# Two unused tiles that move the SBUF pools to multiples of 2048 bytes in a hybrid SSM, convolution and feed-forward layer

## The chip, the cores and the metric

The kernel runs on one core of a Trainium2 chip. The metric is the device time of one execution in microseconds (us), taken as the median over runs. The profile is one execution recorded by the hardware profiler; its times count from the first instruction.

## What is computed

One layer with model width 2048 over 512 positions, in float32, batch 1:

```
h = rms_norm(x, pre_mix_g);  u, v, g = split(h @ w_in)          # 2048 -> 3 x 1024
y_ssm  = s5_mixer(u, ...)          # complex diagonal state space, gelu, y * sigmoid(y @ w_glu)
y_conv = silu(layer_norm(causal_conv31(v * sigmoid(g))))
x = x + rms_norm(concat(y_ssm, y_conv) @ w_out, post_mix_g)     # 2048 -> 2048
h = rms_norm(x, pre_ffn_g)
gate, val = split(causal_conv3(h @ w_up))                       # 2048 -> 2 x 5632
x = x + rms_norm((gelu(gate) * val) @ w_down, post_ffn_g)       # 5632 -> 2048
```

## The kernel before

Activations lie with channels on the 128 partitions and the 512 positions along the free axis, so one tile of 128 channels is 512 float32 numbers, 2048 bytes of each partition. Every large product is done by `gemm`. A weight chunk of 128x1024 float32 (8 blocks of 128x128) is loaded into `wraw`, ScalarE rounds it to fp32r (`wh`, L96) and VectorE takes the rest (`wl`, L97). An activation likewise stands as a high tile and a low tile. For each block TensorE then does three matmuls with 512 columns into one PSUM bank:

```
pe.matmul(ps[m], wh[:, kk, m, :], xh, start=k == 0, stop=False)
pe.matmul(ps[m], wh[:, kk, m, :], xl, start=False, stop=False)
pe.matmul(ps[m], wl[:, kk, m, :], xh, start=False, stop=k == nk - 1)
```

These are L116, L117 and L118. The 512-column operand streamed through the array is called the moving operand; the 128x128 block loaded ahead of it is the weight.

There are 8448 such matmuls. 2112 come before the feed-forward part (input projection, gated linear unit, output projection), with moving tiles in pool `hl16` (name `hl`, slices of 2048 bytes). The feed-forward part has 22 calls for `w_up` with 8 chunks of 24 matmuls, 4224 in all, whose moving tiles are again `hl`; and 44 calls for `w_down` with 2 chunks of 24, 2112 in all, whose moving tiles `hidh` and `hidl` lie in pool `hid`. Calls for `w_up` and `w_down` alternate: after each two `w_up` calls come four of `w_down`.

`wh` and `wl` have two buffers each, `wraw` three. A planner orders the instructions of each engine; weight loads and splits get a higher priority (`WPRI`).

Before the feed-forward part VectorE also does the 31 taps of the convolution (L567), the evacuations and part of the state space work, so that the splits L97 wait in its queue among them. At the end come the last normalization and the stores.

**Where the tiles lie.** Pools are laid one after the other in the order in which they are opened, each tile rounded up to 32 bytes. Ahead of the first lie 16,512 bytes of the program's own. `const` takes 3,808 bytes, so `hl16` starts at 20,320 = 9 x 2048 + 1888. `hl16`, `s16`, `wp` (`wraw`, `wh`, `wl`), `rp` and the first tiles of `t1` (`tmp`) have sizes that are multiples of 2048, so each of their tiles starts at 1888 past a multiple of 2048; a weight block of `wh` or `wl` starts at that plus a multiple of 512. `t1` ends with small tiles (1,152 bytes past a multiple), so the pools behind it, `cp` in the first phase and `hid` in the second, start at 170,976 = 83 x 2048 + 992.

Of the kernel before, what the change touches and what calls it, by code (L numbers as in the profile page):

```python
# [10 lines left out]
F32 = mybir.dt.float32  # L11
# [5 lines left out]
P = 128  # L17
# [39 lines left out]
def layer_kernel(ctx, tc, a, out):  # L57
    nc = tc.nc
    ve, se, ge, pe, sy = nc.vector, nc.scalar, nc.gpsimd, nc.tensor, nc.sync

    const = ctx.enter_context(tc.tile_pool(name="const", bufs=1))
    dram = ctx.enter_context(tc.tile_pool(name="dram", bufs=1, space=bass.MemoryType.DRAM))
    hl16 = ctx.enter_context(tc.tile_pool(name="hl16", bufs=4))
    s16 = ctx.enter_context(tc.tile_pool(name="s16", bufs=2))
# [7 lines left out]
    def tmp():  # L72
        return t1.tile([P, S], F32, name="tmp", bufs=NTMP)
# [53 lines left out]
    def rsqrt_bcast(parts, n, copy=True):  # L127
# [20 lines left out]
        se.copy(out=rb, in_=rps)  # L148
        return rb

    ph1 = ExitStack()
    cp = ph1.enter_context(tc.tile_pool(name="cp", bufs=2, reuse_waits="tile"))

    def k4():
        return cp.tile([P, 1024], F32, name="k4", bufs=3)
# [68 lines left out]
    gpf = cload("post_ffn_g", [P, DK])  # L224
    fcw = cload("ffn_conv_w", [P, 2 * NFF, 3])

    # ---- SSM parameters, states on partitions (group of a pair, state), pairs of groups along the free axis
    uscr = [dram.tile([HC, T, 8, NC], F32, name=f"uscr{m}") for m in range(8)]
    wscr = [dram.tile([2, 16, T, P], F32, name=f"wscr{h}") for h in range(2)]
    bscr = dram.tile([P, 2, NQ, HC], F32, name="bscr")  # L230
# [58 lines left out]
    tt(sh, sh, sh, MUL)  # L289
    ts(sh, sh, -2.0, 1.0, MUL, ADD)  # L290

    # powers of the step: lamr, and lami with the sign turned, by (pair, power)
    lamr = p2.tile([P, NQ, NT], F32, name="lamr")
    lami = p2.tile([P, NQ, NT], F32, name="lami")
    ge.memset(lamr[:, :, 0], 1.0)
# [24 lines left out]
    lpow(1, 2, 2)  # L320
    lpow(1, 3, 4)

    # (step - 1) / eigenvalue
    lr, li = lamr[:, :, 1], sn[:, 0:NQ]
    nr = ts(sm("nr"), lr, -1.0, 1.0, ADD, MUL)
    ab, ab2 = sm("ab"), sm("ab2")
# [20 lines left out]
    tt(tA, tA, tB, SUB)  # L347
    tt(coi, tA, rd, MUL)

    # times powers of the step: columns to rows, and spread over the channels of a group  # L350
    cf = pp.tile([P, 2, NQ, T], F32, name="cf")
    cx = pp.tile([P, NQ, T], F32, name="cx")

# [22 lines left out]
    prep.close()  # L376
    cv = ph1.enter_context(tc.tile_pool(name="cv", bufs=1, reuse_waits="tile"))

    # discretized B
    bsb = k4().rearrange("p (r q h) -> p r q h", r=2, h=HC)  # L380
    bin_ = k4().rearrange("p (r q h) -> p r q h", r=2, h=HC)
    sy.dma_start(out=bin_, in_=a["ssm_b"])
# [12 lines left out]
    for h in range(2):  # L395
# [5 lines left out]
        for mm in range(4):  # L401
# [5 lines left out]
            by = tmp().rearrange("p (q s) -> p q s", q=4)  # L407
# [4 lines left out]
            ve.tensor_tensor(out=w0, in0=w0, in1=bx, op=SUB)  # L412
            ve.tensor_tensor(out=w1, in0=w1, in1=by, op=ADD)

    # C times powers of the step (with the sign of the imaginary part turned)
    for m in range(8):
        ct = cp.tile([P, 2, 4, NT, HC], F32, name="cst", bufs=2)
        cin = p2.tile([P, 2, 4, HC], F32, name="cin")
# [14 lines left out]
            sy.dma_start(out=cscr[m][:, :, gg].rearrange("r p q t -> p r q t"),  # L433
                         in_=ct[PH * gg:PH * gg + PH].rearrange("p r q t h -> p r q (t h)"))

    # ---- input projection: the SSM branch
    def uload(m):
        um = t1.tile([P, S], F32, name="um", bufs=2).rearrange("p (g c) -> p g c", g=8)
        sy.dma_start(out=um, in_=uscr[m].rearrange("h j g c -> (h j) g c"))
        return um  # L440
# [20 lines left out]
    u_evac(pu0, 0)  # L461
    u_evac(gemm(wing[1], xrhs), 4)

    # ---- recurrence over chunks
    ve.memset(st[:, :, :, 0], 0.0)
    lr8 = lam8[:, 0:1, :].broadcast_to([P, 2, NQ])
    for c in range(NC - 1):
# [4 lines left out]
        ve.tensor_tensor(out=sa, in0=sa, in1=st[:, :, :, c + 1], op=ADD)  # L472
        scan_end = ve.tensor_tensor(out=st[:, :, :, c + 1], in0=sa, in1=sx, op=ADD).ins

    # ---- response within a chunk
    kb = s16.tile([P, 4096], F32, name="s16")
    bst = kb[:, 0:1056].rearrange("p (r q h) -> p r q h", r=2, h=HC)
    ge.memset(bst[:, :, NQ, :], 0.0)
# [56 lines left out]
        for i in range(2):  # L535
            sy.dma_start(out=yall[:, m - 1 + i], in_=yscr[m // 2][P * i:P * i + P])

    # ---- input projection: the convolution branch
    csb = cv.tile([P, 8, S], F32, name="csb")

    def vg_evac(ps, i0):
# [28 lines left out]
    for i in range(4):  # L570
        vg_evac(gemm(wing[2 + i], xrhs), 2 * i)

    # ---- SSM branch: operands of the gated linear unit
    yh = hl16.tile([P, 8, S], F32R, name="hl")
    yl = hl16.tile([P, 8, S], F32R, name="hl")
    yc = []
# [4 lines left out]
                         in1=yh[:, m, :].bitcast(F32).rearrange("p (c j) -> p c j", j=T), op=SUB)  # L581
        yc.append(yn)

    # ---- SSM branch: gated linear unit
    zh = hl16.tile([P, 8, S], F32R, name="hl")
    zl = hl16.tile([P, 8, S], F32R, name="hl")
    yrhs = [(yh[:, k, :], yl[:, k, :]) for k in range(8)]
# [10 lines left out]
            se.copy(out=zh[:, m, :], in_=zt)  # L598
            ve.tensor_tensor(out=zl[:, m, :], in0=zt, in1=zh[:, m, :].bitcast(F32), op=SUB)

    # ---- convolution branch: layer norm and swish
    cs = rp.tile([P, S], F32, name="ssq")
    ge.tensor_tensor(out=cs, in0=csb[:, 0], in1=csb[:, 1], op=ADD)
    for i in range(2, 8):
# [21 lines left out]
        se.copy(out=ch[:, i, :], in_=sl)  # L626
        ve.tensor_tensor(out=cl[:, i, :], in0=sl, in1=ch[:, i, :].bitcast(F32), op=SUB)

    # ---- output projection
    yo = [s16.tile([P, 8, S], F32, name="s16") for _ in range(2)]  # L630

    def yt(m):
# [26 lines left out]
    ry = rsqrt_bcast([yss] + last, D, False)  # L659
    ph1.close()  # L660

    # ---- residual, and the norm before the feed-forward part
    hid = ctx.enter_context(tc.tile_pool(name="hid", bufs=8, reuse_waits="tile"))
    t2 = ctx.enter_context(tc.tile_pool(name="t2", bufs=1, reuse_waits="tile"))
    x1scr = dram.tile([P, DK, S], F32, name="x1scr")
# [27 lines left out]
            ge.tensor_tensor(out=xs2, in0=xs2, in1=sq, op=ADD)  # L693
    r2 = rsqrt_bcast([xs2], D)

    # ---- feed-forward part
    fa = [s16.tile([P, 8, S], F32, name="s16") for _ in range(2)]

    def ft(m):
# [150 lines left out]
```

## Time and profile before

| | |
|---|---|
| median of 3 runs | 2148.36 us (2146.53 to 2149.66) |
| profiled execution, span from first to last instruction | 2146.2 us |
| time of the runs' median beyond that span | 2.2 us |
| TensorE busy | 2029.9 us, 95% of the span |
| VectorE busy | 1215.0 us, 57% |
| ScalarE busy | 665.7 us, 31% |
| DMA | 118 GB/s mean |

The profiled execution has its span as its own time; what a run takes beyond it is shown by the third line. Matmuls overlap in the pipeline, so the duration of one (about 0.39 us) is longer than the distance from its start to the start of the next; the distance is what counts.

### The profile page before, as it was taken

Reading aid. Unit: us, or ns where it says so; the run is one execution under the profiler, and the core shown is the slowest. Engines: PE = TensorE matmul, PEld = TensorE weight load, DVE = VectorE, ACT = ScalarE, POOL = GpSimd, SP = SyncE. Lnnn points to the kernel's source line nnn. Section 1 sums busy time; section 2 is a strip of 40 time slices with the busy share of each in tenths; the row PEclk is TensorE's granted clock in tenths of the full one; section 3 lists DMA queues with packets and bytes.
Section 4 is the critical chain, followed back from the end, with each engine's and each line's share of the span. In section 5 each row is a group of like instructions: output and inputs, shape, how many; then the busy total and the mean of one; then the engine's idle time right before and its main releaser. Section 6 shows DMA issues by size and latency. Waiting matters only on the chain.

```text
span 2146.2 us, 23254 instructions
## 1 busy us (share of the span) xinstructions
PE 2029.9 (95%) x9190; PEld 1659.9 (77%) x9190; DVE 1215.0 (57%) x1609; ACT 665.7 (31%) x827; POOL 290.4 (14%) x291
## 2 busy tenths in 40 slices
PE   7767999799997999999999999999999999999995
PEld 6656788677886888888888888888888888888884
DVE  6288999998439552453544535345443464434546
ACT  5111233433535333222312223122231222213233
POOL 6655144303023000000000000000000000000004
PEclk9888999899998999999999999999999999999998
DMA  6785576322423322232223222222232222322242
GB/s 205 170 211 161 202 205 198 95 89 91 174 98 127 109 90 97 98 98 97 91 97 98 98 89 98 98 98 92 96 98 98 98 89 98 98 96 94 95 167 98
DMA packets 111373, 252.36 MB, mean 118 GB/s; under 512 B 28064, under 2 KB 49568, under 8 KB 110752
## 3 DMA queue, kind: packets, MB, share of 16 engines
q1 hardware_dynamic: 106512, 248.77, 36.2%
q10 hardware_dynamic: 4752, 2.11, 0.4%
q8 instruction: 72, 1.18, 0.2%
q14 instruction: 37, 0.30, 0.0%
HBM read 229.67 MB, written 21.17 MB: 117 GB/s over the span
## 4 chain that ended last, share of the span: by engine, by line
PE 72%; DVE 3%; ACT 1%; issue 0%; DVEq 0%; ACTq 0%
PE mm L118 24%; PE mm L116 24%; PE mm L117 24%; DVE hl L685 0%; DVE s L775 0%; DVE s L682 0%; DVE wl L97 0%; DVE hidh L683 0%; PE aux L144 0%; DVE s L776 0%; DVE hidl L683 0%; ACT L137 0%; ACT wh L96 0%; ACT tmp L759 0%; ACT tmp L655 0%
## 5 line engine op out<-in xcount | busy, mean ns | idle before, releaser
L97 DVE TENSOR_TENSOR wl<-wraw,wh 128x1024 fp32r<-128x1024 f32 (+1 forms) x353 | 441.3, 1250 | 777.7 <-ACT wh L96 771.7
L116 PE MATMUL mm<-hl,wh 128*128 128x512 f32 x2112 | 831.9, 395 | 15.2 <-ACT wh L96 9.4
L118 PE MATMUL mm<-hl,wl 128*128 128x512 f32 x2112 | 778.6, 397 | 60.2 <-DVE wl L97 60.2
L117 PE MATMUL mm<-hl,wh 128*128 128x512 f32 x2112 | 831.4, 394 | 0.2 <-DVE hl L685 0.2
L96 ACT CAST wh<-wraw 128x1024 fp32r<-128x1024 f32 (+1 forms) x353 | 370.4, 1050 | 1091.3 <-PE mm L117 1004.7
L118 PEld LDWEIGHTS mm<-hl,wl 128*128 128x128 f32 x2112 | 403.5, 191 | 154.9 <-DVE wl L97 70.1
L116 PEld LDWEIGHTS mm<-hl,wh 128*128 128x128 f32 x2112 | 402.7, 191 | 99.8 <-ACT wh L96 9.8
L117 PEld LDWEIGHTS mm<-hl,wh 128*128 128x128 f32 x2112 | 402.5, 191 | 86.6 <-DVE hl L685 1.4
L117 PE MATMUL mm<-hidl,wh 128*128 128x512 f32 x704 | 277.6, 394 | 0.0
L116 PE MATMUL mm<-hidh,wh 128*128 128x512 f32 x704 | 277.4, 395 | 0.0
L118 PE MATMUL mm<-hidh,wl 128*128 128x512 f32 x704 | 256.6, 395 | 0.0
L761 POOL TENSOR_TENSOR ssq<-ssq,tmp 128x512 f32<-128x512 f32 x11 | 17.3, 1577 | 1394.2 <-ACT tmp L759 1393.7
L567 DVE SCALAR_TENSOR_TENSOR csb<-z,c_conv_w,csb 128x512 f32<-128x512 f32 x210 | 182.9, 930 | 0.0
L116 PEld LDWEIGHTS mm<-hidh,wh 128*128 128x128 f32 x704 | 132.2, 188 | 32.6 <-ACT wh L96 0.5
L118 PEld LDWEIGHTS mm<-hidh,wl 128*128 128x128 f32 x704 | 132.2, 188 | 32.0
L117 PEld LDWEIGHTS mm<-hidl,wh 128*128 128x128 f32 x704 | 132.2, 188 | 31.6
L751 DVE TENSOR_TENSOR s<-mm,s 128x512 f32<-128x512 f32 x160 | 109.9, 691 | 51.1 <-PE mm L118 50.6
L726 DVE SCALAR_TENSOR_TENSOR tmp<-ab,c_ffn_conv_w,tmp 128x512 f32<-128x512 f32 x176 | 125.5, 748 | 0.0
L724 ACT ACTIVATE tmp<-ab,c_ffn_conv_w 128x512 f32<-128x512 f32 x88 | 63.0, 720 | 44.5 <-DVE ab L716 44.5
L716 DVE TENSOR_TENSOR ab<-mm,rr 128x512 f32<-128x512 f32 x88 | 60.4, 689 | 8.2 <-PE mm L118 4.5
L564 POOL TENSOR_TENSOR csb<-csb,pt 128x512 f32<-128x512 f32 x30 | 54.0, 1800 | 53.6 <-ACT pt L563 53.6
L732 ACT CAST hidh<-tmp 128x512 fp32r<-128x512 f32 x44 | 27.2, 621 | 76.6 <-DVE tmp L730 76.6
(212 smaller groups left out, 964.6 us busy)
## 6 DMA issues: line engine op xcount, KB each, us to landing
wraw<-in_ffn_w_up SPq DMA_DIRECT2D x176, 512.0 KB, 3.4
wraw<-in_ffn_w_down SPq DMA_DIRECT2D x88, 512.0 KB, 3.4
wraw<-in_w_in SPq DMA_DIRECT2D x47, 512.0 KB, 5.0
wraw<-in_w_out SPq DMA_DIRECT2D x32, 512.0 KB, 3.4
cst<-cscr SPq DMA_DIRECT2D x16, 576.0 KB, 5.0
cscr<-cst SPq DMA_DIRECT2D x16, 288.0 KB, 4.4
k<-in_ssm_bT SPq DMA_DIRECT2D x8, 512.0 KB, 3.7
um<-uscr SPq DMA_DIRECT2D x16, 256.0 KB, 5.0
```

Of the source, the lines that this page charges most:

```text
L96: se.copy(out=h[:, o], in_=raw[:, o])
L97: ve.tensor_tensor(out=l[:, o], in0=raw[:, o], in1=h[:, o].bitcast(F32), op=SUB)
L116: pe.matmul(ps[m], wh[:, kk, m, :], xh, start=k == 0, stop=False)
L117: pe.matmul(ps[m], wh[:, kk, m, :], xl, start=False, stop=False)
L118: pe.matmul(ps[m], wl[:, kk, m, :], xh, start=False, stop=k == nk - 1)
L564: ge.tensor_tensor(out=csb[:, c, :], in0=csb[:, c, :], in1=pt, op=ADD)
L567: ve.scalar_tensor_tensor(out=csb[:, c, :], in0=zk, scalar=w, in1=csb[:, c, :], op0=MUL, op1=ADD)
L716: ve.tensor_tensor(out=t[:, 2:], in0=ps[j], in1=r2, op=MUL)
L724: se.activation(out=o, in_=t[:, 0:S], func=AF.Copy, scale=fcw[:, c, 0:1])
L726: ve.scalar_tensor_tensor(out=o, in0=t[:, k:k + S], scalar=fcw[:, c, k:k + 1], in1=o, op0=MUL, op1=ADD)
L732: se.copy(out=h, in_=cvt[0])
L751: ve.tensor_tensor(out=ft(m), in0=ps[i], in1=ft(m), op=ADD)
```

## The change

Two pools with one tile each are opened, `lead` with 160 bytes in each partition between `const` and the pools behind it, and `lead2` with 896 bytes behind `t1`. Nothing writes or reads either tile. The pools from `hl16` to `t1` move up by 160 bytes, so that `hl16` starts at 20,480 = 10 x 2048; the pools behind `lead2` move up by 1,056 bytes, to 172,032 = 84 x 2048. `hl`, `wraw`, `wh`, `wl`, `ssq`, `tmp`, `k4` and `hid` tiles then start at multiples of 2048. `um` and `evt`, which lie behind small tiles of `t1`, start at 128 past one; the second `cst` buffer starts at 512 past one; `const` stays where it is. Some comment lines become blank.

```
     const = ctx.enter_context(tc.tile_pool(name="const", bufs=1))
+    lead = ctx.enter_context(tc.tile_pool(name="lead", bufs=1))
+    lead.tile([P, 40], F32, name="lead")
     dram = ctx.enter_context(tc.tile_pool(name="dram", bufs=1, space=bass.MemoryType.DRAM))
     hl16 = ctx.enter_context(tc.tile_pool(name="hl16", bufs=4))
...
+    lead2 = ctx.enter_context(tc.tile_pool(name="lead2", bufs=1))
+    lead2.tile([P, 224], F32, name="lead2")
     ph1 = ExitStack()
     cp = ph1.enter_context(tc.tile_pool(name="cp", bufs=2, reuse_waits="tile"))
```

## Rows read from the trace of the kernel before

**Rows 1.** The page: span, and TensorE's granted clock in 40 slices (tenths).

```profile
span 2146.2 us, 23254 instructions
...
PEclk9888999899998999999999999999999999999998
```

**Rows 2.** The page: chain that ended last, by engine and by line.

```profile
PE 72%; DVE 3%; ACT 1%; issue 0%; DVEq 0%; ACTq 0%
PE mm L118 24%; PE mm L116 24%; PE mm L117 24%; DVE hl L685 0%; DVE s L775 0%; DVE s L682 0%; DVE wl L97 0%; DVE hidh L683 0%; PE aux L144 0%; DVE s L776 0%; DVE hidl L683 0%; ACT L137 0%; ACT wh L96 0%; ACT tmp L759 0%; ACT tmp L655 0%
```

**Rows 3.** Busy time by stretch (start:end, length, engines, granted clock, DMA share, GB/s).

```profile
0.00:500.00 500.00, 420.07 (x2151) 341.04 (x2152) 419.68 (x648) 158.06 (x205) 208.56 (x231) 0.91 0.58 168
500.00:650.00 150.00, 145.34 (x653) 119.79 (x651) 80.78 (x95) 71.06 (x99) 30.76 (x26) 1.00 0.36 123
650.00:712.00 62.00, 52.64 (x219) 41.56 (x220) 52.68 (x67) 28.35 (x44) 23.42 (x15) 0.89 0.40 136
...
760.00:2118.00 1358.00, 1357.98 (x5930) 1112.87 (x5929) 615.15 (x732) 383.59 (x450) 17.34 (x11) 1.00 0.29 98
```

**Rows 4.** Groups by line, 712 to 2118 us: TensorE, `hl` and `hid` matmuls.

```profile
L117 PE MATMUL mm<-hl,wh 128*128 128x512 f32 x1346 | 523.8, 389 | 0.0
...
L117 PE MATMUL mm<-hidl,wh 128*128 128x512 f32 x702 | 276.8, 394 | 0.0
```

**Rows 5.** Timeline of TensorE, `hl` matmuls: first and last of 14.

```profile
760.01 0.39 PE L117 MATMUL mm<-hl,wh 128*128 128x512 f32 x1
...
762.96 0.39 PE L117 MATMUL mm<-hl,wh 128*128 128x512 f32 x1
```

**Rows 6.** Timeline of TensorE, `hid` matmuls: first, second and last of 15 starts.

```profile
936.65 0.39 PE L116 MATMUL mm<-hidh,wh 128*128 128x512 f32 x1
936.88 0.40 PE L117 MATMUL mm<-hidl,wh 128*128 128x512 f32 x1
...
939.92 0.63 PE L118 MATMUL mm<-hidh,wl 128*128 128x512 f32 x2
```

**Rows 7.** Busy time by stretch: one stretch at the lower clock.

```profile
336.50:346.50 10.00, 10.00 (x38) 9.03 (x38) 10.00 (x11) 2.04 (x3) 3.89 (x3) 0.50 0.68 203
```

**Rows 8.** Timeline of TensorE in that stretch, `hl` matmuls: first and last of 9.

```profile
342.83 0.63 PE L116 MATMUL mm<-hl,wh 128*128 128x512 f32 x1
...
346.24 0.57 PE L116 MATMUL mm<-hl,wh 128*128 128x512 f32 x1
```

**Rows 9.** Timeline of TensorE, 64-column matmuls around 336.5 us, first and last.

```profile
335.79 0.28 PE L525 MATMUL aux<-um,k 128*128 128x64 f32 x1
...
336.35 0.60 PE L526 MATMUL aux<-tmp,cst 128*128 128x64 f32 x2
336.74 0.63 PE L525 MATMUL aux<-um,k 128*128 128x64 f32 x2
...
341.43 0.64 PE L526 MATMUL aux<-tmp,cst 128*128 128x64 f32 x2
```

**Rows 10.** Groups by line, TensorE, 0 to 500 us (last column: idle before, releaser).

```profile
L118 PE MATMUL mm<-hl,wl 128*128 128x512 f32 x496 | 190.5, 418 | 51.9 <-DVE wl L97 51.9
```

**Rows 11.** The same, 500 to 650 us.

```profile
L118 PE MATMUL mm<-hl,wl 128*128 128x512 f32 x208 | 74.5, 390 | 3.2 <-DVE wl L97 3.2
```

**Rows 12.** Waits, 712 to 2118 us (total, times, longest).

```profile
ACT wh L96 <- PE mm L117: 809.2, 237, 4.5
DVE wl L97 <- ACT wh L96: 698.9, 201, 4.4
```

**Rows 13.** Groups by line, VectorE, 712 to 2118 us.

```profile
L751 DVE TENSOR_TENSOR s<-mm,s 128x512 f32<-128x512 f32 x158 | 108.5, 691 | 51.1 <-PE mm L118 50.6
L716 DVE TENSOR_TENSOR ab<-mm,rr 128x512 f32<-128x512 f32 x88 | 60.4, 689 | 8.2 <-PE mm L118 4.5 <-ACT rr L148 3.7
L730 DVE TENSOR_TENSOR tmp<-tmp 128x512 f32<-128x512 f32 x44 | 30.3, 691 | 0.1
L734 DVE TENSOR_TENSOR hidl<-tmp,hidh 128x512 fp32r<-128x512 f32 x44 | 30.2, 689 | 9.3 <-ACT hidh L732 9.3
```

More of the change, by code (lines that the diff above doesn't have):

```diff
@@ L61, in layer_kernel @@
     const = ctx.enter_context(tc.tile_pool(name="const", bufs=1))
+    lead = ctx.enter_context(tc.tile_pool(name="lead", bufs=1))
+    lead.tile([P, 40], F32, name="lead")
     dram = ctx.enter_context(tc.tile_pool(name="dram", bufs=1, space=bass.MemoryType.DRAM))
@@ L149, in rsqrt_bcast @@
         return rb
+    lead2 = ctx.enter_context(tc.tile_pool(name="lead2", bufs=1))
+    lead2.tile([P, 224], F32, name="lead2")
     ph1 = ExitStack()
```

## The prediction

> **What bounds the kernel now.** I read the page first. The granted clock is near full in most slices [rows 1], and the chain of work that ended last is made of the three matmul lines of `gemm`, 24% of the span each [rows 2]. The other 28% is mostly the time before 531 us, to which the chain was not followed back.
>
> Then I cut the span into stretches. From 760 to 2118 us TensorE is busy for 1357.98 of 1358.00 us at full clock, VectorE for 615, ScalarE for 384, with a DMA share of 0.29 [rows 3]. The matmul groups there have no idle time before them [rows 4]. So the feed-forward part, two thirds of the time, lasts as long as its matmuls take to follow each other, and nothing else counts. Before 500 us it is mixed: TensorE has 420 us and VectorE 420 us of 500 [rows 3], and 51.9 us of TensorE's idle time end with the split `wl` [rows 10]. From 500 to 650 us TensorE binds again (145 of 150), with 3.2 us of such waits [rows 3, 11].
>
> The change issues no instruction and moves none. It can only act through what an address does to an instruction's time, and the one time that matters is the distance from one matmul to the next. [...]
>
> - moving operand `hl`, full clock: 13 distances from 760.01 to 762.96 us, 2.95/13 = 226.9 ns [rows 5];
> - moving operand `hid`, full clock: 14 distances from 936.65 to 939.92 us, 3.27/14 = 233.6 ns [rows 6];
> [...]
>
> The mean over 760 to 2118 us agrees: 1358/5930 = 229.0 ns [rows 3], against (2 x 226.9 + 233.6)/3 = 229.1.
>
> [...] And `hl` and `hid` matmuls are the same instruction in shape, type, weights and target bank; what differs is where the moving tile lies: 1888 past a multiple of 2048 for `hl`, 992 for `hid`. That place is worth 6.7 ns. [...]
>
> **The change part by part.** `lead` and `lead2` hold 160 and 896 bytes and cost no instruction, no DMA and no wait; there is nothing to hide. Nothing is queued differently on any engine or DMA queue, if the planner's order stays, which I assume.
>
> *Moving operands.* `hl` goes from 1888 to 0, `hid` from 992 to 0. After it no 2048-byte read of either crosses a 2048-byte boundary, where all of them do now. The trace has no 512-column read from such a place, so I bound the distance. Below, by the array: 213.2 ns, half of rows 8. Above, where the excess stays: 226.9 and 233.6. If steps of 6.7 ns are what a bad start adds, an aligned one has none (213.2) or one (about 220). I don't take the lowest: the 64-column matmuls show that not everything halves with the clock. Five distances from 335.79 to 336.35 us give 112 ns at full clock, 22 from 336.74 to 341.43 give 213.2 at half [rows 9], so 112 - 106.6 = 5 ns are left over. I take the middle, 216.7 ns, for both tiles.
>
> The sum by stretch:
>
> - `w_up`: 4224 x (226.9 - 216.7) = 43.1 us. Of these 189 run before 712 us, where TensorE has gaps (52.6 busy of 62, clock 0.89 [rows 3]); their 1.9 us I don't count: 41.2.
> - `w_down`: 2112 x (233.6 - 216.7) = 35.7 us.
> - 500 to 650 us: three lines with about 208 matmuls each [rows 11], 623 x 10.2 = 6.4 us.
> - 0 to 500 us: 1491 matmuls (three lines of about 497 [rows 10]), at most 15.2 us. VectorE is as busy as TensorE there and its splits are what TensorE waits for, so a faster matmul mostly lengthens that wait: bounds 0 and 15.2, I take 4.
>
> Together 87.3 us. 2146.2 - 87.3 = 2058.9; the median of the runs lies 2.2 us above the profiled span, so 2061 us.
>
> *The cover in the feed-forward part.* A chunk of 24 matmuls lasts 24 x 226.9 = 5.4 us and would last 5.2. In it ScalarE and VectorE must split the next chunk; they wait for TensorE to free a buffer for 809.2 us in total, up to 4.5 us at a time [rows 12], so 0.2 us less a chunk starves nobody. What is late next is nothing until chunks get shorter by over 2 us.
>
> *Other engines.* Their tiles move too. VectorE shows the same time for the same operation on tiles with different starts: 691 ns on `s16` tiles at 1888 (L751) and 689 on the `ab` tiles, whose starts step by 32 bytes (L716); 691 within `tmp` at 1888 (L730) and 689 into `hidl` at 992 (L734) [rows 13]. So I put it at nothing; half a per cent either way of its 420 us before 500 us would be 2 us, and in the feed-forward part it is covered.
>
> [...]
>
> [...]
>
> **The rivals.**
>
> *Only the relative place counts.* TensorE reads weights for the next matmul while it streams the present one, and the two reads may disturb each other by how their addresses stand to each other. `hl` (1888) and the weight blocks (1888 plus multiples of 512) already agree modulo 512; `hid` (992) does not. All shift to 0, so `hl` keeps 226.9 and only `hid` gains its step: 2112 x 6.7 = 14.2 us, 2134 us. For it: `hl`, which agrees with the weights, is the faster one. Against it: nothing, but the excess of `hl` itself is then left without a cause in the address.
>
> [...]
>
> *Slower.* With moving tile, `wh` and `wl` all at 0, both reads begin on the same place, and that may be a worse one than 1888: if `hl` takes the three steps of `hid`, (4224 + 623) x 6.7 = 32.5 us, with some 3 us of the stretch before 500 us, 2184 us. It decides as soon as an aligned `hl` is above 226.9 ns by more than `hid` gains, and for the whole from about 1 ns. Against it: today's equal starts are the faster case.
>
> **How the numbers follow.** The forecast, an absolute gain from aligned starts, gets 0.43; the gain of `hid` alone 0.19; no effect 0.25; slower 0.11; 0.02 is left for a small gain of another kind. The forecast's own range goes from 213.2 ns with all of the stretch before 500 us (57.9 + 43.1 + 8.5 + 20.4, less 2.6, is 127 us: 2021) to 220 ns with none of it (29.1 + 28.7 + 4.3 - 1.3 = 60.8: 2088); a likely stretch of it is 2030 to 2088. The range must also hold the gain of `hid` alone and no effect, so it runs from 2030 to 2150, and leaves out the slower case and the far low end. About 0.2%, 4 us, is what a measurement here can tell from nothing. Faster by more than that: 0.43 + 0.19 + 0.01 = 0.63; within: 0.25; slower: 0.12.
>
> **What would show it.** In the profile after, the timeline between 760 and 2000 us gives each step: the distance of `hl` matmuls (213 to 220 right; 226.9 the second or third case), that of `hid` matmuls (the same as `hl` right; 233.6 no effect), and the unchanged 426 ns at the lower clock. The matmul groups of the feed-forward part should still show no idle time; if `wl` or `wh` waits appear there, the cover was wrong. Idle time before L118 in the first 500 us should grow by most of 15 us. VectorE's means should stay within 1%. The prediction is wrong if the distance of `hl` does not move: then the place of a tile is not what costs the 13.7 ns.

## The result, and the profile after

The changed kernel takes 2129.71 us (median of 4 runs, 2128.84 to 2131.21) beside 2147.45 us before (the three runs of the table above and a fourth): a ratio of 0.9914, 95% interval 0.9900 to 0.9928. It is 18 us faster. The forecast was 2061 us; the rival "only the relative place counts" had 2134.

The page of the kernel after. The added lines move the matmul lines by two: L116 to L118 are now L118 to L120, and L97 is L99.

```profile
span 2128.0 us, 23254 instructions
```

Busy time by stretch, kernel after (start:end, length, then TensorE, weight loads, VectorE, ScalarE, GpSimd, granted clock, DMA share, GB/s):

```profile
0.00:500.00 500.00, 420.57 (x2175) 338.94 (x2176) 430.34 (x656) 159.52 (x206) 205.71 (x231) 0.94 0.56 169
...
760.00:2100.00 1340.00, 1339.97 (x5912) 1109.50 (x5911) 609.58 (x726) 381.40 (x447) 17.41 (x11) 1.00 0.30 99
```

TensorE is again busy without a gap from 760 us on. The mean distance from matmul to matmul there is 1340/5912 = 226.7 ns, where it was 229.0 [rows 3]. The timeline tells which of the two kinds of matmul gained. Kernel after, TensorE: first and last of 9 `hl` starts at the lower clock, of 16 `hl` starts at the full clock and of 19 `hid` starts:

```profile
110.12 0.63 PE L118 MATMUL mm<-hl,wh 128*128 128x512 f32 x1
...
113.53 0.54 PE L118 MATMUL mm<-hl,wh 128*128 128x512 f32 x1
...
759.83 0.39 PE L118 MATMUL mm<-hl,wh 128*128 128x512 f32 x1
...
763.23 0.39 PE L118 MATMUL mm<-hl,wh 128*128 128x512 f32 x1
...
932.77 0.39 PE L118 MATMUL mm<-hidh,wh 128*128 128x512 f32 x1
...
936.85 0.39 PE L119 MATMUL mm<-hidl,wh 128*128 128x512 f32 x1
```

At the lower clock (granted 0.50 from 110.12 to 113.53 us) 3.41/8 = 426 ns, as in [rows 8]. At the full clock (granted 1.00) `hl` has 3.40/15 = 226.7 ns: it was 226.9 [rows 5], so the move from 1888 to 0 did nothing for it. `hid` has 4.08/18 = 226.7 ns: it was 233.6 [rows 6]. It lost its step and stands where `hl` stands. Over all 2100 `hid` distances behind 760 us that the traces hold, the means are 233.3 ns before and 226.7 ns after, so the step is worth 2112 x 6.6 = 14 us.

The other 4 us are gone before the feed-forward part: the reduction for the norm ahead of it starts at 700.15 us, before at 704.19. Timeline of TensorE, kernel before and kernel after:

```profile
704.19 0.95 PE L131 MATMUL aux<-ones,ssq 128*128 128x1 f32 x8
```

```profile
700.15 0.95 PE L133 MATMUL aux<-ones,ssq 128*128 128x1 f32 x8
```

Most of them appear at one wait. Around 86 us VectorE stops for the spread coefficients of the state space part, 16 loads of 256 KB from `wscr` into an `s16` and a `csb` tile; the splits `wl` queue behind it and TensorE waits for them. Waits from 60 to 145 us (total, times, longest), kernel before and kernel after:

```profile
DVE tmp L408 <- DMA s<-wscr: 20.4, 1, 20.4
```

```profile
DVE tmp L412 <- DMA csb<-wscr: 16.6, 1, 16.6
```

DMA issues (count, KB each, median us from issue to landing), kernel before and kernel after:

```profile
s<-wscr SPq DMA_DIRECT2D x8, 256.0 KB, 9.8
csb<-wscr SPq DMA_DIRECT2D x8, 256.0 KB, 10.7
```

```profile
s<-wscr SPq DMA_DIRECT2D x8, 256.0 KB, 8.2
csb<-wscr SPq DMA_DIRECT2D x8, 256.0 KB, 8.7
```

The same loads land 1.6 and 2.0 us sooner each, and the wait is 3.8 us shorter. The wait of TensorE for `wl` in the first 500 us became shorter, 44.1 us where [rows 10] has 51.9, but that for `wh` became longer, 14.6 us where it was 9.4; together they lost 2.6 us. Groups by line, TensorE, 0 to 500 us, kernel before and kernel after:

```profile
L116 PE MATMUL mm<-hl,wh 128*128 128x512 f32 x498 | 202.7, 409 | 12.9 <-ACT wh L96 9.4 <-DVE evt L447 3.6
```

```profile
L118 PE MATMUL mm<-hl,wh 128*128 128x512 f32 x506 | 206.0, 409 | 21.0 <-ACT wh L98 14.6 <-DVE evt L451 3.5 <-DVE evt L550 2.9
...
L120 PE MATMUL mm<-hl,wl 128*128 128x512 f32 x504 | 191.0, 413 | 44.2 <-DVE wl L99 44.1
```

TensorE's granted clock over these 500 us rose as well, from 0.91 [rows 3] to 0.94. Whether that is a part of the 4 us or follows from the changed waits was not separated.

### The profile page after: what moved, and what is told of

Read it like the earlier page. It is cut to its first block, busy times and chain, and to the rows that moved or that the text cites. A ratio compares the mean times of both kernels' runs of the same rounds, so it can differ in the third digit from the quotient of the medians.

```text
span 2128.0 us, 23254 instructions
## 1 busy us (share of the span) xinstructions
PE 2012.5 (95%) x9190; PEld 1654.4 (78%) x9190; DVE 1218.9 (57%) x1609; ACT 666.3 (31%) x827; POOL 287.6 (14%) x291
## 4 chain that ended last, share of the span: by engine, by line
PE 72%; DVE 3%; ACT 1%; issue 0%; DVEq 0%; ACTq 0%
PE mm L120 24%; PE mm L118 24%; PE mm L119 24%; DVE hl L689 0%; DVE s L779 0%; DVE s L686 0%; DVE wl L99 0%; DVE hidh L687 0%; PE aux L146 0%; DVE s L780 0%; DVE hidl L687 0%; ACT L139 0%; ACT wh L98 0%; ACT tmp L763 0%; ACT tmp L659 0%
## 5 line engine op out<-in xcount | busy, mean ns | idle before, releaser
L99 DVE TENSOR_TENSOR wl<-wraw,wh 128x1024 fp32r<-128x1024 f32 (+1 forms) x353 | 447.6, 1268 | 772.1 <-ACT wh L98 766.1
L118 PE MATMUL mm<-hl,wh 128*128 128x512 f32 x2112 | 832.7, 395 | 23.3 <-ACT wh L98 14.6
L120 PE MATMUL mm<-hl,wl 128*128 128x512 f32 x2112 | 777.5, 396 | 52.5 <-DVE wl L99 52.5
L120 PEld LDWEIGHTS mm<-hl,wl 128*128 128x128 f32 x2112 | 402.5, 191 | 148.1 <-DVE wl L99 64.1
L118 PEld LDWEIGHTS mm<-hl,wh 128*128 128x128 f32 x2112 | 402.8, 191 | 108.6 <-ACT wh L98 15.4
L118 PE MATMUL mm<-hidh,wh 128*128 128x512 f32 x704 | 273.2, 389 | 0.0
L120 PE MATMUL mm<-hidh,wl 128*128 128x512 f32 x704 | 252.6, 389 | 0.0
L765 POOL TENSOR_TENSOR ssq<-ssq,tmp 128x512 f32<-128x512 f32 x11 | 17.4, 1583 | 1380.6 <-ACT tmp L763 1380.0
L118 PEld LDWEIGHTS mm<-hidh,wh 128*128 128x128 f32 x704 | 132.1, 188 | 27.9 <-ACT wh L98 0.5
L120 PEld LDWEIGHTS mm<-hidh,wl 128*128 128x128 f32 x704 | 132.2, 188 | 27.5
L568 POOL TENSOR_TENSOR csb<-csb,pt 128x512 f32<-128x512 f32 x30 | 49.3, 1645 | 60.4 <-ACT pt L567 60.4
```

The source lines that it names most:

```text
L99: ve.tensor_tensor(out=l[:, o], in0=raw[:, o], in1=h[:, o].bitcast(F32), op=SUB)
L568: ge.tensor_tensor(out=csb[:, c, :], in0=csb[:, c, :], in1=pt, op=ADD)
```

## The experiments

After the result two things were to be settled: whether it is the place of the moving operand relative to the weights that costs the 6.6 ns, or its own place; and what makes the 13 ns by which 226.7 stands above 213 ns, half of the 426 ns at clock 0.50 (the author's estimate of the distance at clock 1.00). The ratios below are to runs of the kernel before that were made beside each version. Their medians lie between 2147.0 and 2149.8 us, so differences of 3 to 5 us between versions run at different times are uncertain by about 3 us.

**The distance by itself.** One group of 96 matmuls after another, without the layer. `M(o)` is 512 columns of one fp32r tile from column `o`, `W(i, o)` the weight block number i mod 8 of another, `o` columns late; both tiles start at a multiple of 2048, and 8 columns are 32 bytes. Some of the 36 groups:

```
    for i in range(NM): pe.matmul(p[:, 0:512], W(i, 0), M(0), ...)      # L107
    for i in range(NM): pe.matmul(p[:, 0:512], W(i, 0), M(8), ...)      # L111
    for i in range(NM): pe.matmul(p[:, 0:512], W(i, 0), M(16), ...)     # L115
    for i in range(NM): pe.matmul(p[:, 0:512], W(i, 0), M(32), ...)     # L123
    for i in range(NM): pe.matmul(p[:, 0:512], W(i, 0), M(64), ...)     # L131
    for i in range(NM): pe.matmul(p[:, 0:512], W(i, 32), M(0), ...)     # L183
    for i in range(NM): pe.matmul(p[:, 0:512], W(i, 64), M(0), ...)     # L187
    for i in range(NM): pe.matmul(p[:, 0:512], W(i, 8), M(8), ...)      # L195
    for i in range(NM): pe.matmul(p[:, 0:512], W(i, 32), M(32), ...)    # L199
    for i in range(NM): pe.matmul(p[:, 0:512], W(i, 0), M(1), ...)      # L211
    for i in range(NM): pe.matmul(p[:, 0:512], W(i, 1), M(0), ...)      # L219
    for i in range(NM): pe.matmul(p[:, 0:512], wb[...], mb[:, 0:512], ...)   # L231, bf16
    for i in range(NM): pe.matmul(p[:, 0:512], wb[...], mb[:, 64:576], ...)  # L235, bf16
```

> The disputed cost by itself: 36 groups of 96 matmuls, each group one combination of where the moving operand and the weight blocks start (bytes past a multiple of 2048; weight blocks step by 512), without the layer: nothing of the reference is computed but some products. Theory A (the place of the moving operand relative to the weight block, modulo 512, sets the distance): 226.9 ns at equal starts, wherever both stand (0 and 0, 32 and 32, 128 and 128, 480 and 480), 233.4 ns with the moving operand 128 bytes ahead, and the same values whether the moving operand or the weights are moved by the opposite amount. Theory B (the moving operand's own start): moving the weights alone changes nothing, and a common shift changes the distance as a shift of the moving operand alone does. Theory C (a fixed price of fp32r at the high clock): no fp32r combination goes below 226.9 ns, and bf16 operands do, at about 216 ns. If A or B can reach the array's own pace, some combination shows 213 to 217 ns.

Groups by line of this kernel (busy us, mean ns of one); the distance is the busy time less the last matmul, over 95, good to about 0.5 ns:

```profile
L111 PE MATMUL mm<-mv,wt 128*128 128x512 f32 x96 | 22.6, 395 | 0.0
...
L123 PE MATMUL mm<-mv,wt 128*128 128x512 f32 x96 | 22.6, 395 | 0.0
...
L183 PE MATMUL mm<-mv,wt 128*128 128x512 f32 x96 | 22.5, 395 | 0.0
...
L115 PE MATMUL mm<-mv,wt 128*128 128x512 f32 x96 | 22.1, 391 | 0.0
...
L199 PE MATMUL mm<-mv,wt 128*128 128x512 f32 x96 | 22.0, 390 | 0.0
L195 PE MATMUL mm<-mv,wt 128*128 128x512 f32 x96 | 22.0, 389 | 0.0
...
L131 PE MATMUL mm<-mv,wt 128*128 128x512 f32 x96 | 21.9, 389 | 0.0
L187 PE MATMUL mm<-mv,wt 128*128 128x512 f32 x96 | 21.9, 389 | 0.0
...
L107 PE MATMUL mm<-mv,wt 128*128 128x512 f32 x96 | 21.9, 389 | 0.0
...
L231 PE MATMUL mm<-mb,wb 128*128 128x512 bf16 x96 | 20.9, 379 | 0.0
```

Equal starts give (21.9 - 0.39)/95 = 226 ns (L107), and equal starts that are 32 or 128 off give 227 (L195, L199): a common shift does nothing. A shift of the moving operand alone by 32 or 128 bytes gives 234 (L111, L123), of the weights alone by 128 gives 233 (L183). So it is the difference that counts. A difference of 256 bytes, on either side, is as good as none (L131, L187), so the period is 256 bytes here and not the 512 of the expectation; 64 bytes lie between, 229 (L115). A moving operand four bytes ahead costs most, 237 ns (L211); weights four bytes ahead cost 232 (L219). No plain fp32r read of 512 columns in this kernel went below 226 ns; bf16 has 216 ns, at equal starts (L231) and with 128 bytes of difference (L235).

**One filler at a time.**

```
-    lead = ctx.enter_context(tc.tile_pool(name="lead", bufs=1))
-    lead.tile([P, 40], F32, name="lead")
```

leaves `lead2` alone, and

```
-    lead2 = ctx.enter_context(tc.tile_pool(name="lead2", bufs=1))
-    lead2.tile([P, 224], F32, name="lead2")
```

leaves `lead` alone.

> Only the second filler: hl16, wh and wl stay at 1888, hid goes from 992 to 1888, all off a multiple of 2048. Theory A (relative place): hid and weights agree, so the whole gain of the change, 2130 to 2134 us, hid distance 226.7 ns. Theory B in the form that a multiple of 64 or more is needed: hid stays at 233.4 ns and the time at 2147 us.

> Only the first filler: hl16, wh and wl at 0, hid at 1152, which is 128 past a multiple of 512, as it is relative to the weights in the kernel before. Theory A: hid stays at 233.4 ns, time 2143 to 2148 us. Theory B (own start, with 992 bad because it is 32 past a multiple of 64): hid at 226.7 ns and 2130 us.

`lead2` alone: 2134.26 us, ratio 0.9931 (0.9917 to 0.9946). `lead` alone: 2146.05 us, 0.9984 (0.9975 to 0.9993). Busy time by stretch, `lead2` alone, then `lead` alone:

```profile
760.00:2100.00 1340.00, 1339.97 (x5912) 1109.13 (x5911) 612.10 (x730) 383.24 (x449) 17.43 (x11) 1.00 0.30 99
```

```profile
760.00:2100.00 1340.00, 1339.99 (x5852) 1098.26 (x5852) 607.44 (x723) 375.48 (x438) 9.33 (x6) 1.00 0.30 99
```

With nothing at a multiple of 2048, but `hid` at 1888 like the weights, the mean distance is 226.7 ns, all that the change gains in the feed-forward part. With everything in the first pools at 0 and `hid` 128 past, it is 1340/5852 = 229.0, as before. The relative theory (theory A) held both times. What the first lacks to the changed kernel, 4.5 us, and what the second has over the kernel before, 3.7 us, point to the transfers: the loads from `wscr` land in 9.5 and 10.1 us in the first, in 8.0 and 8.2 in the second. The profile of the second does not show its gain: in the profiled run, the slowest of ten, the reduction for the norm starts at 703.32 us, 0.9 us sooner than before.

**The weights alone.** The changed kernel with `wh` and `wl` in a pool of their own between two fillers:

```
+    wlead = ctx.enter_context(tc.tile_pool(name="wlead", bufs=1))
+    wlead.tile([P, 32], F32, name="wlead")
+    wq = ctx.enter_context(tc.tile_pool(name="wq", bufs=2))
+    wend = ctx.enter_context(tc.tile_pool(name="wend", bufs=1))
+    wend.tile([P, 96], F32, name="wend")
...
-    lead2.tile([P, 224], F32, name="lead2")
+    lead2.tile([P, 96], F32, name="lead2")
```

> The changed kernel with wh and wl alone moved to 128 past a multiple of 512, all moving operands still at multiples of 512. Theory A: both hl and hid now stand apart from the weights, both go to about 233.4 ns or another value than 226.7; at 233.4 the feed-forward part costs 6336 x 6.6 = 42 us more and the rest 3 to 10, so 2175 to 2182 us. Theory B (moving operand's own start): 226.7 ns and 2130 us, as the changed kernel.

2168.80 us, 1.0090 (1.0073 to 1.0107): the only version slower than the kernel before, with `hl` and `hid` still at multiples of 2048. Busy time by stretch:

```profile
760.00:2100.00 1340.00, 1340.00 (x5768) 1086.57 (x5767) 595.89 (x707) 360.38 (x417) 0.00 (x0) 1.00 0.30 98
```

The mean distance is 1340/5768 = 232.3 ns. 6336 x (232.3 - 226.7) = 35 us of the 39 us over the changed kernel lie in the feed-forward part. The moving operand's own start is refuted as the cause. The expectation was 6 us too long because 233.4 was taken for 232.3.

**Everything 32 bytes further, and only the pools of the landing tiles.** Two edits of the changed kernel. The first moves every pool from `hl16` on. The second moves `s16` and the pool that holds `csb` (and other tiles of the convolution) by 32 bytes, and `wp`, `rp` and `t1` by 256:

```
-    lead.tile([P, 40], F32, name="lead")
+    lead.tile([P, 48], F32, name="lead")
```

```
+    s16a = ctx.enter_context(tc.tile_pool(name="s16a", bufs=1))
+    s16a.tile([P, 8], F32, name="s16a")
     s16 = ctx.enter_context(tc.tile_pool(name="s16", bufs=2))
+    s16b = ctx.enter_context(tc.tile_pool(name="s16b", bufs=1))
+    s16b.tile([P, 56], F32, name="s16b")
...
-    lead2.tile([P, 224], F32, name="lead2")
+    lead2.tile([P, 160], F32, name="lead2")
...
+    cva = ph1.enter_context(tc.tile_pool(name="cva", bufs=1, reuse_waits="tile"))
+    cva.tile([P, 8], F32, name="cva")
```

> The changed kernel with every pool from hl16 on moved by 32 more bytes: all tiles agree with each other modulo 256 as in the changed kernel, but none starts at a multiple of 64. Relative theory: hl and hid distances stay at 226.7 ns; if the rest of the gain (about 4 us before 650 us) comes from where transfers land, it is lost: 2133 to 2135 us. If aligned starts as such matter to TensorE: distances above 226.7 ns and 2147 us or more.

> The changed kernel with only s16 and the pool that holds csb moved by 32 bytes (weights and tmp end 256 past a multiple of 2048). Relative theory with a period of 256: hl distance still 226.7 ns. If the 4 us of the early part come from the 16 loads of the spread coefficients into s16 and csb, their landing time goes back from 8.2 and 8.7 us to about 9.8 and 10.7 us, the early part loses 3 to 5 us, and the time is 2133 to 2135 us; if other transfers or the weights do it, the time stays at 2130 us.

Everything 32 bytes further: 2134.28 us, 0.9938 (0.9925 to 0.9952). Only the pools of `s16` and `csb`: 2133.41 us, 0.9935 (0.9921 to 0.9949). The matmuls are untouched in both. Busy time by stretch of the first, then of the second, with the second's DMA issues and VectorE's wait from 60 to 145 us:

```profile
760.00:2100.00 1340.00, 1339.96 (x5912) 1109.12 (x5911) 614.68 (x733) 383.49 (x451) 14.94 (x10) 1.00 0.30 99
```

```profile
760.00:2100.00 1340.00, 1339.97 (x5912) 1109.14 (x5911) 610.92 (x728) 382.85 (x449) 17.42 (x11) 1.00 0.30 99
```

```profile
s<-wscr SPq DMA_DIRECT2D x8, 256.0 KB, 8.9
csb<-wscr SPq DMA_DIRECT2D x8, 256.0 KB, 10.0
```

```profile
DVE tmp L418 <- DMA csb<-wscr: 17.4, 1, 17.4
```

Moving the pools of the two tiles in which these loads land gives back 3.7 us of the 4 and raises the landing times to 8.9 and 10.0 us. So the early gain seems to go with where these pools start, though the intervals of the two runs and of the changed kernel overlap. That it comes through the one wait at 86 us is not shown: here that wait is 17.4 us, near the 16.6 of the changed kernel, and yet the time is longer. `csb` starts at 320 past a multiple of 2048 in the changed kernel, and its loads land in 8.7 us there, so for the landing a multiple of 64 was enough and 2048 was not needed.

**What the other 13 ns are.** The same kind of kernel, with offsets between, shorter moving operands and repeated columns; some of its groups:

```
    for i in range(NM): pe.matmul(..., W(i, 0), M(0), ...)                                    # L103
    for i in range(NM): pe.matmul(..., W(i, 0), mv[:, 0:1].broadcast_to([P, 512]), ...)       # L135
    for i in range(NM): pe.matmul(..., wt[:, 0:1].broadcast_to([P, 128]), M(0), ...)          # L139
    for i in range(NM): pe.matmul(p[0:128, 0:256], W(i, 0), M(0, 256), ...)                   # L175
    for i in range(NM): pe.matmul(p[0:128, 0:256], W(i, 0), M(32, 256), ...)                  # L179
    for i in range(NM): pe.matmul(p[0:128, 0:128], W(i, 0), M(0, 128), ...)                   # L183
```

> Groups of 96 matmuls alone, without the layer (only products of parts of the input are computed), for two questions. First, the fine offsets: with the moving operand 48, 80, 112, 144, 176, 208 or 240 bytes ahead of the weights, the relative theory with a period of 256 expects 229 to 235 ns and never under 226.7. Second, the 13.4 ns that stay at equal starts. Theory F (a fixed price of each fp32r matmul, whatever is read): 226.7 ns also where the moving operand or the weight block is one column repeated, and 13.4 ns over the array's pace for 384, 256 and 128 columns. Theory G (the two reads disturb each other even at equal starts): a repeated column on either side takes the distance to about 216 ns, and weight blocks of 64 or 32 columns take it part of the way.

```profile
L139 PE MATMUL mm<-mv,wt 128*128 128x512 f32 x96 | 22.4, 394 | 0.0
...
L103 PE MATMUL mm<-mv,wt 128*128 128x512 f32 x96 | 21.9, 389 | 0.0
...
L135 PE MATMUL mm<-mv,wt 128*128 128x512 f32 x96 | 21.2, 381 | 0.0
...
L175 PE MATMUL mm<-mv,wt 128*128 128x256 f32 x96 | 11.7, 283 | 0.0
L179 PE MATMUL mm<-mv,wt 128*128 128x256 f32 x96 | 11.6, 281 | 0.0
...
L183 PE MATMUL mm<-mv,wt 128*128 128x128 f32 x96 | 10.8, 275 | 0.0
```

With 256 columns the distance is (11.7 - 0.28)/95 = 120 ns, again 13 ns over the estimate (half of 213), and with 384 columns 173 ns, again 13 over it (160; L167). The distance grows by 53 ns for each 128 columns, a quarter of 213. So from 256 columns on the 13 ns are a price of each matmul and not of each column. At 128 columns the expectation failed: the distance is 111 ns (L183), 58 over the estimate, and what sets it there was not looked into. The price of the place is another: 128 bytes of difference cost 7 ns at 512 columns, 3 at 384 (L171) and nothing at 256 (119 ns, L179).

The 13 ns are no fixed price either: one moving column repeated takes the distance to 219 ns (L135). Repeating the weight column instead gives 232 (L139), no better than a bad offset, and weight blocks of 64 and 32 columns don't take it down either (22.2 and 22.4 us for 96). The seven finer offsets lie between 231 and 236 ns. Neither theory held as it was put: the price changes with how the moving operand is read, and does not fall with the amount of weights.

So other orders of reading were tried. The first kernel of that kind showed 595 ns for every group, the plain one too, with the granted clock at 1.00:

> Groups of 96 matmuls alone (only products of parts of the input are computed), all at equal starts, with other ways to read the same amount. A moving operand of one repeated column took the distance from 226.7 to 218.7 ns, so the question is which part of the moving read costs the 8 ns. If it is going on to new addresses in steps of 256 bytes, repeating a piece of up to 64 columns (256 bytes) stays near 218.7 and pieces of 128 and 256 columns show 226.7. [...] If the order of the two reads matters, a moving operand with its halves swapped, or weights read with a stride, differ from 226.7 by 2 ns or more in either direction; a form below 220 ns at unrepeated data would be worth some 40 us in the layer. Cycling over four banks should change nothing.

```profile
L103 PE MATMUL mm<-mv,wt 128*128 128x512 f32 x96 | 57.4, 828 | 0.0
```

It tells nothing of the patterns. The same kernel run again, and one with fewer patterns, showed the plain group at 226 to 227 ns, so it was not the kernel; what it was stays open.

```
    for i in range(NM): pe.matmul(..., W(i, 0), mv[:, 0:4].unsqueeze(1).broadcast_to([P, 128, 4]), ...)  # L107
...                                                                                                      # L111: 16 columns, L119: 64
    for i in range(NM): pe.matmul(..., wt[:, 0:1024].rearrange("p (c s) -> p c s", s=8)[:, :, i % 8], M(0), ...)  # L131
    for i in range(NM): pe.matmul(ps4[i % 4], W(i, 0), M(0), ...)                                        # L135
```

> The same question with plain forms only: groups of 96 matmuls alone at equal starts, in which the moving operand is a piece of 4, 16, 32, 64, 128 or 256 columns read again and again up to 512 columns, then weights read with a stride of 8 columns, then four banks in turn. In the run before, every group stood at 595 ns a matmul, the plain one too, which no group of two other kernels of this kind showed; here the plain group must show 226.7 ns to be read at all. Then: 218.7 ns for repeated pieces up to 256 bytes and 226.7 above it if going on to new steps of 256 bytes is the price; 226.7 ns already for a piece of 16 columns if it is the plain stream.

```profile
L131 PE MATMUL mm<-mv,wt 128*128 128x512 f32 x96 | 23.8, 409 | 0.0
L111 PE MATMUL mm<-mv,wt 128*128 128x512 f32 x96 | 23.4, 405 | 0.0
...
L119 PE MATMUL mm<-mv,wt 128*128 128x512 f32 x96 | 22.0, 389 | 0.0
L135 PE MATMUL mm<-mv,wt 128*128 128x512 f32 x96 | 22.0, 389 | 0.0
...
L107 PE MATMUL mm<-mv,wt 128*128 128x512 f32 x96 | 21.2, 381 | 0.0
```

A piece of 64 columns (256 bytes) repeated costs what the whole tile costs, 227 ns; 16 columns repeated cost more, 242 ns; 4 columns 219 ns. Four banks in turn change nothing. So going on to new steps of 256 bytes is not the price. The reading of the weights counts too: with every eighth column as weight the distance is 246 ns (L131). The kernel with all patterns:

```
    ... mv[:, 0:512].rearrange("p (a b) -> p a b", a=2)[:, ::-1, :] ...   # L135: halves swapped
    ... mv[:, 0:512].rearrange("p (a b) -> p b a", a=2) ...               # L139: 0, 256, 1, 257, ...
    ... mv[:, 0:512].rearrange("p (a b) -> p b a", b=2) ...               # L143: 0, 2, 4, ..., 1, 3, ...
```

> The kernel with all patterns once more. If 595 ns a matmul came from the chip at that moment, the plain group shows 226.7 ns now and the patterns can be read: halves swapped, eight pieces in backward order, alternate columns, every second column. If this kernel itself causes it, 595 ns again in all groups.

```profile
L143 PE MATMUL mm<-mv,wt 128*128 128x512 f32 x96 | 43.7, 632 | 0.0
...
L135 PE MATMUL mm<-mv,wt 128*128 128x512 f32 x96 | 21.9, 389 | 0.0
...
L139 PE MATMUL mm<-mv,wt 128*128 128x512 f32 x96 | 20.9, 379 | 0.0
```

Halves swapped: 226 ns, no change, and none with eight pieces in backward order (L159). Every second column: 453 ns, twice as long. Columns taken in turn from the two halves: (20.9 - 0.38)/95 = 216 ns, as bf16 has. Alignment alone did not reach that.

**In the layer.** The changed kernel with this order in `gemm`; the products lie in that order in PSUM, and each instruction that reads them from there puts them back:

```
+    def halves(t):
+        return t.rearrange("p (a b) -> p b a", a=2)
...
-                    pe.matmul(ps[m], wh[:, kk, m, :], xh, start=k == 0, stop=False)
+                    pe.matmul(ps[m], wh[:, kk, m, :], halves(xh), start=k == 0, stop=False)
...
-        return ps
+        return [p.rearrange("p (b a) -> p a b", a=2) for p in ps]
...
-                ve.tensor_tensor(out=t[:, 2:], in0=ps[j], in1=r2, op=MUL)
+                ve.tensor_tensor(out=nat(t[:, 2:]), in0=ps[j], in1=nat(r2), op=MUL)
```

`nat(t)` is `t` seen as two halves of 256. The second kernel is the same edit of the kernel before.

> The changed kernel in which each large product reads its moving tile alternately from its two halves (columns 0, 256, 1, 257, ...); the products lie in that order in PSUM and the instruction that reads them from there puts them back. Alone, this order took the distance from 226.7 to 215.8 ns. If it does so in the layer: 6336 x 10.9 = 69 us less in the feed-forward part, some 7 us less between 500 and 650 us and 0 to 8 before, so 2046 to 2056 us. If the reads of PSUM with a step of two columns are slow enough to make VectorE or ScalarE late, idle time before the matmuls appears and the gain is smaller.

> The same order of reading in the kernel before, without fillers. If the place relative to the weights costs only a plain read, hid and hl both show 215.8 ns and the time is 2050 to 2060 us; if it costs this order too, hid stays some 6.6 ns above hl and the time is about 14 us longer than that of the other run of this pair, plus 4 us for the transfers.

With the fillers: 2053.36 us, 0.9553 (0.9538 to 0.9567). Without: 2060.24 us, 0.9585 (0.9568 to 0.9602). Busy time by stretch, with, then without:

```profile
760.00:2020.00 1260.00, 1259.80 (x5836) 1102.54 (x5835) 602.93 (x720) 373.86 (x441) 14.70 (x10) 1.00 0.31 104
```

```profile
760.00:2020.00 1260.00, 1259.80 (x5836) 1102.52 (x5835) 599.88 (x716) 370.06 (x435) 11.30 (x7) 1.00 0.31 105
```

Both have 1260/5836 = 215.9 ns: with this order the place relative to the weights costs nothing any more, though `hid` stands at 992 and the weights at 1888 in the second. The 7 us between them are therefore not the matmuls of this stretch. In the two profiles 5.2 us of the difference are there when the reduction for the norm starts (692.48 us with, 697.72 without). The loads from `wscr` land in 7.9 and 8.3 us with the fillers and in 9.5 and 11.0 without, which fits the 4 us above; that the difference comes through VectorE's wait for them is not shown, and the early part was not taken apart further. The reads of PSUM with a step cost nothing: L727, which is L716 before, has 686 ns (689 in [rows 13]). Groups of VectorE by line, with the fillers, 712 to 2024 us:

```profile
L727 DVE TENSOR_TENSOR ab<-mm,rr 128x512 f32<-128x512 f32 x84 | 57.6, 686 | 2.4
```

This version beats both kernels.

## Why the prediction was wrong

The direction was right, and its main mechanism was not.

*What bounds the kernel* was right: the feed-forward part lasts as its matmuls follow each other, and no other engine became late (no idle time there at 229 or 226.7 ns, and 0.2 us of 1260 at 215.9 ns).

*Moving operands* is the step that failed: "I take the middle, 216.7 ns, for both tiles". The distances were read rightly, and the difference between `hl` and `hid` was rightly put down to where they lie. The lower bound, 213.2 ns, is the author's estimate, half of the 426.3 ns at clock 0.50 [rows 7, 8]; `hl` lies 13.7 ns above it, about two steps of 6.7 ns, and `hid` three. The error was to take this excess of `hl` for two more steps of the same kind. `hl` had no step left: it already agreed with the weights modulo 256, and 1888 was as good a start as 0. So the term of `w_up`, 41.2 us, and that of 500 to 650 us, 6.4 us, were nothing, and the term of `w_down`, 35.7 us, was 14. The runs put in its place: a difference between the starts of moving operand and weight block that is no multiple of 256 bytes costs 2 to 10 ns a matmul of 512 columns (229 to 237 ns beside 226.7). No run shows 213.2 ns, nor 216.7 for a plain fp32r read: those stayed at 226 ns or more, and 215.9 ns came only when the moving operand was read from its two halves in turn. The measured 2130 us lies inside the stated range only because that was drawn to hold the gain of `hid` alone and no effect as well; the forecast's own stretch, 2030 to 2088 us, missed it.

*The rival "only the relative place counts"* had the cause and the price (14.2 us), with a period of 512 that the run put at 256. It said that nothing spoke against it; what spoke for it was in the text already: `hl` agrees with the weights and is the faster, `hid` does not and is the slower, and that one cause explains their difference without a second step for `hl`.

*Other engines* was right for VectorE in the feed-forward part (its four groups are within 1% of [rows 13]); over the whole execution the splits `wl` went from 1250 to 1268 ns each, 1.4% more, for a reason that no run looked for. And the part left out the transfers altogether. Tiles in which transfers land moved as well, and at 86 us VectorE stood in a wait of 20 us for such a transfer, with the splits behind it. The pools of those tiles go with the 4 us by which even the rival was short. The wait for `wl` in the first 500 us fell by 8 us where it was forecast to grow by most of 15; that growth hung on faster `hl` matmuls, which did not come. Where they did come, with the columns in turn and the fillers, it is 58.3 us, 6.4 more than before. The 4 us that the sum has for that stretch are right in size by chance: they were to come from faster matmuls.

*The slower rival* asked whether equal starts are the worse place. They are the better one; unequal ones are slower, as the run with the weights alone shifted shows (232.3 ns).

Open are three things: why reading from two halves in turn removes the price, why a moving piece of 16 columns repeated costs 242 ns, and by which waits the 4 us before the feed-forward part come about. The runs give the numbers and no mechanism. The traces show weight loads running while matmuls do (1109.50 us and 1339.97 us busy in the 1340.00 us from 760 us on, kernel after). That the disturbance is between these two reads of the memory was argued from the period of 256 bytes, not shown.

## What to carry to other kernels

When one instruction has two distances in one trace, look at what differs between its operands' places, and first at their places relative to each other; then move one operand at a time, because a common shift shows nothing. In fp32r products where TensorE never idles, let moving tiles of 512 columns and weight blocks start alike modulo 256 bytes (226.7 ns here, 229 to 237 otherwise; at 256 columns it made no difference, 120 and 119 ns), or read the moving tile from its two halves in turn, which here is worth more (4.1% without the fillers, 4.5% with them) and made the place indifferent to the matmuls (215.9 ns with and without the fillers). When tiles are moved, go through the transfers that land in them too, above all those for which an engine waits.

## What the runs showed of the hardware

- At clock 0.50 `hl` matmuls have 426 ns for 512 columns before and after; at clock 1.00 plain fp32r reads have 226.7 ns at equal starts modulo 256 bytes and 229 to 237 otherwise, and bf16 216 ns.
- Plain fp32r reads at equal starts have 120 ns for 256 columns, 173 for 384, 226.7 for 512: 53 ns for each 128 columns, and 13 ns a matmul over the estimate of half the time at clock 0.50. 128 columns have 111 ns.
- The price of 128 bytes of difference shrinks with the columns: 7 ns at 512, 3 at 384, nothing at 256.
- fp32r columns read in turn from the halves of the tile: 216 ns. Every second column of a tile: 453 ns. Every eighth column as weight: 246 ns.
- Loads of 256 KB from device memory landed in 7.9 to 8.7 us (medians of eight) in tiles that start at a multiple of 64 bytes, and in 8.9 to 11.0 us in tiles 32 bytes past one.
- VectorE read PSUM with a step of two columns in the time of a plain read (686 and 689 ns).
